# Retention in a hybrid decoder on one core: k of two heads and two gate tiles computed ahead, rotations behind the last norm, and a job's two loads swapped

## The chip, the core and the metric

The kernel runs on one core of one Trainium2 chip. The metric is the device time of one execution in microseconds (us). Five engines work side by side, each through its own instructions in order: TensorE (PE in the profile: matmuls; PEld: its weight loads), VectorE (DVE), ScalarE (ACT), GpSimd (POOL) and SyncE (SP, which here only issues DMAs). ACT and POOL issue a few DMAs as well. An engine that waits for a semaphore holds up everything behind it in its own order.

## The reference, cut to what matters

One step of a decoder of two layers, for 512 prompt tokens and 8 x 4 sample tokens together (544 columns, `T`; `HT` is half of it). Layer 0 mixes by a short gated convolution, layer 1 by retention with 4 heads (`NH`); behind each mixer stands a gated feed-forward network (FFN).

```
def retention_mixer(x, s0, pos, w_in, gn_g, w_out):
    z = x @ w_in
    q, k, v, g = jnp.split(z, [QK_DIM, 2 * QK_DIM, 2 * QK_DIM + V_DIM], axis=-1)
    ...
    q = rotary(q, pos)
    k = rotary(k, pos) * (HEAD_DK ** -0.5)
    o, S = retention_chunkwise(q, k, v, s0)
    of = (of - mu) * lax.rsqrt(var + GN_EPS)
    ...
    out = (jax.nn.silu(g) * of.astype(x.dtype)) @ w_out
```

A head has 256 columns of q and of k (2 pieces of 128 each) and 512 of v and of the gate g (4 gate tiles of 128).

## The kernel before, in words

Activations lie transposed: 128 features on the partitions, 544 tokens along the row. Every fp32 operand is split into a high and a low part (`split`, L191: ACT writes the high part, DVE subtracts), and a product takes three matmuls: high x high, high x low, low x high. Where `split_adding` or `mixed` is used, the low part of some weights is made by a DMA from POOL's queue that adds the weights to the negated high part.

Two forms of a projection stand beside each other. `project` (its matmuls are L175) takes one piece of 128 output columns: 8 row blocks x 3 x 2 halves = 48 matmuls of 272 columns. A `Job` (L461 and on, its matmuls L480) computes two pieces with a scheme of seven products (after Strassen and Winograd): 7 x 4 x 3 = 84 matmuls of 272 columns. Its operands on the activation side are sums made once; on the weight side, `weights7` (L428) loads two blocks, `w3` (L434) and then `w1` (L435), and forms sums on DVE (L438 needs only `w3`, L439 both) that are then split. The seven products go into three banks of PSUM: `begin` makes product 1 and takes it (`u1`), `middle` products 6, 5 and 2 (`u2`, `c11`), then 7 (`u3`, `c22`), `end` the products 4 and 3 (`c21`, `c12`). Each "take" is a small step of ACT (L540 and others) or DVE (L543) that reads a bank, so that it can be written again. `run` (L516) calls, for each job, `prepare` of the next one, `middle`, `begin` of the next one, `end`.

The program has these stages: the convolution; FFN 0, a long chain of jobs; `ahead` (L785); retention, head by head; FFN 1; the final norm. `ahead` computes, still in the pools of FFN 0, what retention needs first: k and q of head 0 by `project`, stored unrotated to DRAM (`qk_made`), and gate tiles as jobs, stored finished to DRAM (`gate_made`): two of head 0, and all four of heads 1 and 2 (`AHEAD`), 5 jobs.

Then the tables `gt` (the decay factors of a head) and the raw k and q of head 0 (`rot`) are loaded back (`qk_start`, L915; `qk_loaded`, L926), issued on SP's queue after `last_load`, the last load of the jobs. DVE scales (L942, L930) and rotates them (`rotate`, L969 to L974: six steps of 128 x 544 for one of q and k).

A head runs so:

- `value` (L987): v in four weight pieces (`c`), each of 24 matmuls of 512 columns (L999 to L1001); behind each odd piece four small matmuls for the sample tokens (L1007). Behind the second piece stand the splits of q and k (`qk_split`), `sample_scores`, the transposes of k (`keys`: L1049, L1058), and, in heads 1 and 2, the split of the previous head's gated output (`held_parts`).
- `fill(0)` to `fill(3)`: blocks of projections between the steps of the recurrence. In heads 1 and 2 these are the output projection of the previous head (`held_project`), in head 0 its gate tiles 2 and 3 and k of head 1, in head 3 its own four gate tiles (`gate_project`).
- `scores`, the sample tokens' states (`sample_outputs`, `states_update`: DVE steps S, L1243), and the outputs of the four chunks (`inner`), each normalized over its 512 columns (`normalized`: mean and variance on DVE, a power on POOL for the reciprocal root, L227, and `yn`, L1148), transposed by PE (L1172) and multiplied into the gate (`gated`, L1178).
- Among these stand projections of the next head: in head 0 both pieces of q of head 1; in heads 1 and 2 the two pieces of k of the next head, and behind the last norm (`yn3`) and its transposes the two pieces of q. A rotation follows the second piece at once. The second piece holds, in its middle (`inside`), a state update and the transposes of `yn2`.
- Head 3 has no next head: its places are taken by the output projection of head 2 (pieces 4 and 5, then 2 and 3 about the last norm), and `last_project` ends the stage.

The order on each engine is written by the order of the calls, with `issue_after` placing a group behind a given instruction; a scheduler and the pools' free slots decide the rest. PE's order is therefore fixed when the program is built.

The functions that the change touches:

Of the kernel before, what the change touches and what calls it, by code (L numbers as in the profile page):

```python
# [12 lines left out]
P = 128  # L13
# [36 lines left out]
def hybrid_decode_kernel(ctx: ExitStack, tc: tile.TileContext, a: dict, o: dict):  # L50
# [79 lines left out]
    last_load = [None]  # L130
# [297 lines left out]
    def weights7(src1, src2, sw, adding=False):  # L428

        n = KP * P  # L430
        w3, w1 = [wts.tile([P, 2 * n], F32, tag="w", name=nm("w")) for _ in range(2)]
        w2 = sw.tile([P, 2 * n], F32, tag="w2", name=nm("w2"))
        w4 = sw.tile([P, n], F32, tag="w4", name=nm("w4"))
        last_load[0] = nc.sync.dma_start(w3, src2)  # L434
        last_load[0] = nc.sync.dma_start(w1, src1)  # L435
# [347 lines left out]
    gate_made = {h: dram.tile([P, 4, T], F32, tag=f"g{h}", name=nm("gm")) for h in (0, *AHEAD)}  # L783

    def ahead(tp, fp, sw, operand_tiles):  # L785

# [46 lines left out]
        def gates(h, n):  # L833
# [28 lines left out]
    with ExitStack() as c2:  # L862
# [47 lines left out]
        def qk_start(h):  # L910

            st = {}
            gt = kp.tile([P, 2, T], F32, tag="gt", name=nm("gt"), bufs=1)
            with tc.issue_after(last_load[0].ins) if h == 0 else ExitStack():
                nc.sync.dma_start(gt, a["gtab"][h])  # L915
            st["gt"] = gt
            st["rot"] = [
                pool.tile([P, 2, T], F32, tag=f"rot{w}", name=nm("rot"), bufs=1) for w, pool in enumerate((tp, kp))
            ]
            return st  # L920

        def qk_loaded(st):

            for t, src in ((st["rot"][1], qk_made[1]), (st["rot"][0], qk_made[0])):
                with tc.issue_after(last_load[0].ins):
                    nc.sync.dma_start(t, src)  # L926
# [16 lines left out]

        def qk_project(h, st, which, dt, inside=None):
# [42 lines left out]
        def value(h, st):  # L987
# [4 lines left out]
            for c in range(4):  # L992
# [19 lines left out]
                if c == 1:  # L1012
# [89 lines left out]
        def gate_project(h, st, n):  # L1102
            st.setdefault("gate", [])
            if h == NH - 1 and n % 2 == 0:

                pool, tag = ((kp, "gt"), (qp, "qkhl1"))[n // 2]
                t = pool.tile([P, 2, T], F32, tag=tag, name=nm("gate"), bufs=1)
                st["gate"].append(t)
            elif not st["gate"]:
                st["gate"].append(swapped(True, [P, 4, T], F32, "gate"))  # L1110
# [27 lines left out]

        def normalized(src, tag="yn"):
# [8 lines left out]
            nc.vector.tensor_scalar(yn, src, mv[:, 0:1], rs, op0=ALU.subtract, op1=ALU.mult)  # L1148
# [149 lines left out]
        for h in range(NH):  # L1298
            more = h + 1 < NH

            def fill(n):
# [4 lines left out]
                elif h:  # L1306
                    gate_project(h, st, n)
# [3 lines left out]
                else:  # L1311
                    qk_project(h + 1, nxt, 1, n - 2)

# [24 lines left out]
            if not more:  # L1338
                held_parts(h, older)
# [6 lines left out]
            if more and h:  # L1346
                nxt = qk_start(h + 1)
                for which in (1, 0):
                    qk_scale(nxt, which)
# [27 lines left out]
            if more and h:  # L1377
                qk_project(h + 1, nxt, 0, 0)
                qk_project(h + 1, nxt, 0, 1)
# [122 lines left out]
```

## Time and profile before

| | |
|---|---|
| Median of 3 runs | 1458.5 us (1458.18 to 1458.96) |
| Profiled execution | 1461.27 us |
| Its span, first to last instruction | 1459.5 us |
| Mean granted TensorE clock | 0.996 |
| PE busy | 1443.8 us (99%) |
| DVE, ACT, POOL busy | 985.7, 664.0, 147.9 us |
| Bytes moved by DMA | 201.89 MB, mean 138 GB/s |

The profile was taken in one execution, whose own time is 2.8 us above the median of the runs; times inside the trace are measured against its span. The columns of the rows quoted below are: in the list of waits, the engine and line that waited, what it waited for, the total, the number and the longest; in the busy times by stage, the stretch, then for each engine the busy time and number of instructions, the granted clock, the DMA share and GB/s; in the timelines, start, duration, engine, line, operation, output tile <- input tiles, shape, and in brackets the idle time ahead of it and what ended it. The matmuls' durations overlap: what a matmul costs is the distance from one start to the next.

### The profile page before, as it was taken

The numbers are of one execution on the slowest core, as the hardware profiler recorded it, in microseconds if no ns is written. First come the engines' busy times: TensorE is split into PE (matmuls) and PEld (weight loads), VectorE is DVE, ScalarE is ACT, GpSimd is POOL, SyncE is SP. The second block draws the span as 40 slices with busy tenths as digits, with TensorE's granted clock in tenths as the row PEclk, the third lists the DMA queues.
The fourth block names the chain that finished last, engine by engine and source line by source line (L and its number), as shares of the span: only waits on it lengthen the run. The fifth ranks groups of instructions, "written<-read, shape, count | busy, mean of one in ns | idle before, by whom it ended". The sixth has DMA issues, their size and how long they took to land.

```text
span 1459.5 us, 26302 instructions
## 1 busy us (share of the span) xinstructions
PE 1443.8 (99%) x10860; PEld 1369.0 (94%) x10860; DVE 985.7 (68%) x1536; ACT 664.0 (45%) x971; POOL 147.9 (10%) x184
## 2 busy tenths in 40 slices
PE   9999999999999999999999999999999999999997
PEld 8999999999999999997878888878999999999997
DVE  5644679847748648677575765845699848749554
ACT  5222466626526437664223032134386626537334
POOL 0100011101101003210010000000111101101002
PEclk9999999999999999999999999999999999999998
DMA  6222246636536434767353734724666635546432
GB/s 219 82 88 92 86 114 140 150 116 126 143 106 139 124 80 133 195 167 262 125 191 116 258 106 144 274 92 143 175 138 149 153 108 131 131 109 148 119 81 77
DMA packets 84297, 201.89 MB, mean 138 GB/s; under 512 B 8129, under 2 KB 25409, under 8 KB 83921
## 3 DMA queue, kind: packets, MB, share of 16 engines
q1 hardware_dynamic: 67296, 165.91, 35.9%
q0 software_dynamic: 15008, 29.18, 12.2%
q10 hardware_dynamic: 1872, 5.12, 0.9%
q8 instruction: 85, 1.39, 0.4%
q14 instruction: 36, 0.29, 0.1%
HBM read 175.11 MB, written 25.08 MB: 137 GB/s over the span
## 4 chain that ended last, share of the span: by engine, by line
PE 89%; DVE 5%; DMA 3%; ACT 1%; issue 1%; POOL 0%; SPq 0%; DVEq 0%; ACTq 0%; POOLq 0%
PE sm L480 35%; PE mm L175 33%; PE sm L175 7%; PE sm L999 2%; PE sm L1000 2%; PE sm L1001 2%; PE sm L163 2%; PE sm L164 1%; PE sm L165 1%; PE sm L1222 1%; DMA w<-in_ffgu_dram 1%; DVE wl L191 1%; DMA w<-in_rtg_dram 1%; DVE S L1243 1%; DVE ol L191 1%
## 5 line engine op out<-in xcount | busy, mean ns | idle before, releaser
L190 ACT ACTIVATE wh<-w 128x1024 fp32r<-128x1024 f32 (+4 forms) x126 | 115.8, 923 | 318.8 <-PE mm L175 204.9
L480 PE MATMUL sm<-oh,wh 128*128 128x272 f32 x744 | 215.5, 290 | 0.1
L480 PE MATMUL sm<-ol,wh 128*128 128x272 f32 x744 | 214.3, 288 | 0.7 <-DVE ol L191 0.7
L480 PE MATMUL sm<-oh,wl 128*128 128x272 f32 x744 | 213.9, 287 | 0.0
L175 PE MATMUL mm<-xh,wh 128*128 128x272 f32 x844 | 176.3, 290 | 1.1 <-ACT wh L190 1.0
L175 PE MATMUL mm<-xh,wl 128*128 128x272 f32 x844 | 174.5, 289 | 0.4 <-DMA wl<-in_rtqk_dram 0.4
L175 PE MATMUL mm<-xl,wh 128*128 128x272 f32 x844 | 173.9, 287 | 0.0
L480 PE MATMUL sm<-oh,h 128*128 128x272 f32 x568 | 164.1, 289 | 0.5 <-DVE gate L543 0.4
L480 PE MATMUL sm<-oh,l 128*128 128x272 f32 x568 | 163.5, 288 | 0.0
L480 PE MATMUL sm<-ol,h 128*128 128x272 f32 x568 | 163.5, 288 | 0.0
L273 DVE TENSOR_TENSOR x<-x,mm 128x544 f32<-128x544 f32 x90 | 64.7, 719 | 144.7 <-PE mm L175 144.7
L191 DVE TENSOR_TENSOR wl<-w,wh 128x1024 fp32r<-128x1024 f32 (+4 forms) x126 | 134.2, 1071 | 23.7 <-ACT wh L190 22.3
L480 PEld LDWEIGHTS sm<-oh,wh 128*128 128x128 f32 x744 | 139.8, 188 | 2.1 <-ACT gate L540 0.9
L423 ACT ACTIVATE wh<-w 128x1024 fp32r<-128x1024 f32 x97 | 102.8, 1060 | 83.2 <-PE sm L480 56.1
L480 PEld LDWEIGHTS sm<-ol,wh 128*128 128x128 f32 x744 | 139.8, 188 | 0.9 <-DVE ol L191 0.9
L480 PEld LDWEIGHTS sm<-oh,wl 128*128 128x128 f32 x744 | 140.3, 189 | 0.0
L426 POOL DMA_DIRECT2D wl<-in_ffgu_dram x87 | 75.6, 869 | 635.2 <-ACT wl L425 261.5
L175 PEld LDWEIGHTS mm<-xh,wh 128*128 128x128 f32 x844 | 132.2, 188 | 5.4 <-ACT wh L190 1.4
L175 PEld LDWEIGHTS mm<-xh,wl 128*128 128x128 f32 x844 | 131.6, 188 | 0.9 <-DMA wl<-in_rtqk_dram 0.6
L175 PEld LDWEIGHTS mm<-xl,wh 128*128 128x128 f32 x844 | 132.1, 188 | 0.1
L191 DVE TENSOR_TENSOR l<-w,h 128x1024 fp32r<-128x1024 f32 x98 | 93.4, 955 | 27.0 <-ACT h L190 26.4
L480 PEld LDWEIGHTS sm<-oh,h 128*128 128x128 f32 x568 | 107.2, 189 | 1.0 <-ACT wh L423 0.6
(296 smaller groups left out, 3211.8 us busy)
## 6 DMA issues: line engine op xcount, KB each, us to landing
w<-in_ffgu_dram SPq DMA_DIRECT2D x88, 512.0 KB, 3.9
wl<-in_ffgu_dram POOLq DMA_DIRECT2D x87, 256.0 KB, 4.8
w<-in_ffdn_dram SPq DMA_DIRECT2D x96, 192.0 KB, 2.5
S<-in_rets_dram SPq DMA_DIRECT2D x16, 1024.0 KB, 7.0
out_rets_dram<-S SPq DMA_DIRECT2D x16, 1024.0 KB, 4.8
w<-in_cvin_dram SPq DMA_DIRECT2D x21, 512.0 KB, 3.4
w<-in_rtqk_dram SPq DMA_DIRECT2D x16, 512.0 KB, 3.6
w<-in_rtg_dram SPq DMA_DIRECT2D x16, 512.0 KB, 4.1
```

Source lines behind the costliest of these rows:

```text
L163: nc.tensor.matmul(out, lh, rh, start=start, stop=False, skip_group_check=True)
L164: nc.tensor.matmul(out, lh, rl, start=False, stop=False, skip_group_check=True)
L175: last_product[0] = nc.tensor.matmul(half(pt, hf)[:, :HT], w[:, c], act[k][:, hf * HT : (hf + 1) * HT], start=(first and k == ks[0] and i ...
L190: h = nc.scalar.activation(dh, src, AF.Copy)
L191: last_low[0] = nc.vector.tensor_sub(dl, src, dh.bitcast(F32))
L273: last_residual[0] = nc.vector.tensor_add(xk, xk, p)
L423: nc.scalar.activation(wh, w, AF.Copy)
L426: nc.gpsimd.dma_start(wl[:, n:], src[:, n:], accum_op=ALU.add)
L480: last = nc.tensor.matmul(out, w[:, c], b, start=(first and k == 0 and i == 0), stop=(k == KP - 1 and i == 2), skip_group_check=True,)
L999: nc.tensor.matmul(out, xh[kt][:, ts_], wh[:, cw], start=(kt == 0), stop=False)
L1000: nc.tensor.matmul(out, xh[kt][:, ts_], wl[:, cw], start=False, stop=False)
L1001: last = nc.tensor.matmul(out, xl[kt][:, ts_], wh[:, cw], start=False, stop=(kt == KT - 1))
```

## The change

- Three more jobs in `ahead`: k of head 2, k of head 3 (`gates(h, None)`: weights of k in place of those of two gate tiles, the raw sums stored to `k_made`), and gate tiles 0 and 1 of head 3. The list is (0,0), (1,0), (1,2), (2,k), (2,0), (2,2), (3,k), (3,0): 8 jobs.
- Heads 1 and 2 project only q of the next head (two pieces, where k stood). The next head's `gt` and raw k are loaded behind `fill(3)`; behind the last norm (`last_norm`, the DVE step of `yn3`) k is scaled and rotated (`k_loaded`), and then q is rotated, in head 0 too.
- Head 3 computes only its gate tiles 2 and 3, in fills 0 and 1. Fill 2 is empty; fill 3 has the split of head 2's gated output and the output pieces 2 and 3, which stood about the last norm.
- In `value`, the splits of q and k, `sample_scores`, `keys` and `held_parts` stand behind the third weight piece, not the second.
- `weights7` loads `w1` first and `w3` second. `gt` and the raw k of head 0 are issued after the last job's first load (`second_load`), q after its second.

Counted over the program: PE has 10646 matmuls in place of 10682, SP 385 DMA issues in place of 382, ACT's queue 16 in place of 13, POOL's 111 in place of 105.

```diff
     def weights7(src1, src2, sw, adding=False):
...
-        w3, w1 = [wts.tile([P, 2 * n], F32, tag="w", name=nm("w")) for _ in range(2)]
+        w1, w3 = [wts.tile([P, 2 * n], F32, tag="w", name=nm("w")) for _ in range(2)]
...
+        second_load[0] = nc.sync.dma_start(w1, src1)
         last_load[0] = nc.sync.dma_start(w3, src2)
-        last_load[0] = nc.sync.dma_start(w1, src1)
...
+            def k(what, src):
+                g = tile2()
+                if what == "c21":
+                    nc.scalar.activation(g[:, 1, :HT], src, AF.Copy)
+                elif what == "c12":
+                    nc.scalar.dma_start(k_made[h], g)
+
+            if n is None:
+                return Job([a["rtqk"][h, 2 + i] for i in range(2)], operand, sw, summed(tile2, k))
             return Job([a["rtg"][h, n + i] for i in range(2)], operand, sw, summed(tile2, gate))
 
-        jobs = [gates(0, 0)] + [gates(h, n) for h in AHEAD for n in (0, 2)]
+        jobs = [gates(*hn) for hn in ((0, 0), (1, 0), (1, 2), (2, None), (2, 0), (2, 2), (3, None), (3, 0))]
...
-            with tc.issue_after(last_load[0].ins) if h == 0 else ExitStack():
+            with tc.issue_after(second_load[0].ins) if h == 0 else ExitStack():
                 nc.sync.dma_start(gt, a["gtab"][h])
...
-                with tc.issue_after(last_load[0].ins):
+                with tc.issue_after((second_load if src is qk_made[1] else last_load)[0].ins):
                     nc.sync.dma_start(t, src)
...
+        def k_loaded(h, st):
+
+            r = st["rot"][1]
+            nc.vector.tensor_mul(r, r, st["gt"][:, 1, :].unsqueeze(1).to_broadcast([P, 2, T]))
+            rotate(r, *products())
...
-            if dt:
+            if dt and which:
                 rotate(r, *products())
...
-                if c == 1:
+                if c == 2:
                     qk_split(h, st, 1)
                     qk_split(h, st, 0)
                     sample_scores(h, st)
...
-                elif h:
-                    gate_project(h, st, n)
                 elif n < 2:
 
                     gate_project(h, st, n + 2)
-                else:
+                elif more:
                     qk_project(h + 1, nxt, 1, n - 2)
+                elif n == 3:
+                    held_parts(h, older)
+                    held_project(h, 2)
+                    held_project(h, 3)
...
             if h in AHEAD:
                 st["gate"] = [swapped(h == 2, [P, 4, T], F32, "gate")]
                 nc.sync.dma_start(st["gate"][0], gate_made[h])
-            if not more:
-                held_parts(h, older)
+                if more:
+                    nxt = qk_start(h + 1)
+                    nc.sync.dma_start(nxt["rot"][1], k_made[h + 1])
+                    for which in (1, 0):
+                        qk_scale(nxt, which)
+            elif not more:
+                st["gate"][0] = qp.tile([P, 2, T], F32, tag="qkhl1", name=nm("gate"), bufs=1)
+                nc.sync.dma_start(st["gate"][0], gate_made[h][:, :2, :])
...
-                    qk_project(h + 1, nxt, int(h > 0), 0)
+                    qk_project(h + 1, nxt, 0, 0)
...
-                qk_project(h + 1, nxt, int(h > 0), 1, inside)
+                qk_project(h + 1, nxt, 0, 1, inside)
             else:
                 held_project(h, 5, single=True)
                 inside()
-                held_project(h, 2, single=True)
             yn3 = normalized(p3)
-            if not more:
-                held_project(h, 3)
+            if more:
+
+                with tc.issue_after(last_norm[0].ins):
+                    if h:
+                        k_loaded(h + 1, nxt)
+                    rotate(nxt["rot"][0], *products())
             gated_pair(h, st, (yns, 4), (yn3, 3))
-            if more and h:
-                qk_project(h + 1, nxt, 0, 0)
-                qk_project(h + 1, nxt, 0, 1)
```

More of the change, by code (lines that the diff above doesn't have):

```diff
@@ L782, in hybrid_decode_kernel @@
     qk_made = [dram.tile([P, 2, T], F32, tag=f"qk{w}", name=nm("qkm")) for w in range(2)]
[L783 removed]
+    k_made = {h: dram.tile([P, 2, T], F32, tag=f"k{h}", name=nm("km")) for h in range(2, NH)}
+    gate_made = {h: dram.tile([P, 4, T], F32, tag=f"g{h}", name=nm("gm")) for h in range(NH)}
     def ahead(tp, fp, sw, operand_tiles):
@@ L1102, in gate_project @@
         def gate_project(h, st, n):
[L1103 to L1110, printed above, removed]
+            if n == 2:
+                last = h == NH - 1
+                t = kp.tile([P, 2, T], F32, tag="gt", name=nm("gate"), bufs=1) if last else swapped(True, [P, 4, T], F32, "gate")
+                st["gate"] = [None, t] if last else [t]
             wh, wl = load_piece(a["rtg"][h, n], KT * P)
```

9 lines of the change are left out of this document (3 added, 6 removed).

## Prediction

> **What bounds the kernel now.** I read the head of the page first, then the list of PE's waits, then the busy times by stage; the chain of waits and the timelines serve for single terms.
>
> ```profile
> span 1459.5 us, 26302 instructions
> PE 1443.8 (99%) x10860; PEld 1369.0 (94%) x10860; DVE 985.7 (68%) x1536; ACT 664.0 (45%) x971; POOL 147.9 (10%) x184
> ```
>
> ```profile
> PE sm L480 <- DVE gate L543: 2.2, 2, 1.8
> PE sm L309 <- DVE expo L103: 1.1, 1, 1.1
> PE mm L175 <- ACT wh L190: 1.0, 1, 1.0
> PE mm L175 <- DMA wl<-in_rtqk_dram: 0.4, 1, 0.4
> ```
>
> TensorE is busy 99% of the span, and the waits shown (us in total, times, longest) come to 4.7 us of some 5.7 named. So time comes from two places only: fewer matmuls, or more and fewer of those waits. The largest wait (L480 on L543) lies in the stage with the jobs that this change lengthens.
>
> ```profile
> core 0: us, PE busy (x) PEld busy (x) DVE busy (x) ACT busy (x) POOL busy (x), PEclk, DMA share, GB/s
> 205.00:548.00 343.00, 342.87 (x2734) 342.22 (x2735) 239.01 (x363) 176.07 (x265) 37.86 (x43) 1.00 0.51 124
> 582.00:655.00 73.00, 70.46 (x534) 68.51 (x533) 52.76 (x86) 48.50 (x76) 11.86 (x12) 0.98 0.69 184
> 760.00:863.00 103.00, 102.92 (x667) 85.30 (x666) 66.84 (x100) 25.75 (x34) 3.60 (x5) 1.00 0.49 166
> ```
>
> These are the first FFN, the stage with the jobs ahead of retention, and the second head. Only the middle one has idle time (2.5 us) and a granted clock under 1. The head has next to none, so whatever starts to wait there is new.
>
> **The gain: 36 matmuls.** A projection of 48 matmuls a piece becomes half a job of 84 for two pieces. Three pairs move: 3 x 96 go, 3 x 84 come. From the chain:
>
> ```profile
> 40.20 11.95 PE sm L175 x96
> 328.48 63.15 PE sm L480 x504
> ```
>
> 11.95/96 = 0.1245 us in a projection, 63.15/504 = 0.1253 in a job. So 288 x 0.1245 - 252 x 0.1253 = **4.3 us less**. That is all the change can take from TensorE's work; about 31.6 us of job work now stands ahead of the heads.
>
> **The jobs ahead.** The largest wait, by SP, DVE and PE:
>
> ```profile
> 625.85 0.33 SPq L435 DMA_DIRECT2D w<-in_rtg_dram  x1
> 626.23 0.43 SPq L915 DMA_DIRECT2D gt<-in_gtab_dram  x1
> 626.70 0.42 SPq L926 DMA_DIRECT2D rot<-qkm  x1
> ```
>
> ```profile
> 629.65 0.69 DVE L439 TENSOR_TENSOR w<-w,w 128x512 f32<-128x512 f32 x1 [1.18 <-DMA w<-in_rtg_dram]
> 631.24 1.36 DVE L942 TENSOR_TENSOR gt<-gt,R 128x544 f32<-128x544 f32 x2 [0.29 <-DMA gt<-in_gtab_dram]
> 633.19 1.29 DVE L930 TENSOR_TENSOR rot<-rot,gt 128x1088 f32<-128x1088 f32 x1 [0.59 <-DMA rot<-qkm]
> 634.40 0.43 DVE L543 TENSOR_TENSOR gate<-gate,sm 128x272 f32<-128x272 f32 x1
> ```
>
> ```profile
> 632.80 0.29 PE L480 MATMUL sm<-oh,wl 128*128 128x272 f32 x1
> 634.88 0.39 PE L480 MATMUL sm<-xh,h 128*128 128x272 f32 x1 [1.80 <-DVE gate L543]
> ```
>
> ```profile
> 636.00:638.00 2.00, 2.00 (x12) 2.00 (x11) 1.75 (x5) 0.63 (x1) 0.02 (x1) 0.51 0.90 130
> 638.00:640.00 2.00, 2.00 (x12) 2.00 (x12) 2.00 (x3) 1.32 (x2) 0.00 (x0) 0.64 0.27 48
> ```
>
> DVE runs in order: its take of a product (L543) stood behind steps that waited for gt and rot. From start to start PE lost 634.88 - 632.80 - 0.125 = 1.96 us. Then the granted clock falls to 0.51 and 0.64 over two stretches of 2 us: 2 x 0.49 + 2 x 0.36 = 1.7 us of clock (counted by matmul starts 1.55, which I take; a half clock lasting 3.4 us fits both). The two waits of 0.4 us in the list (the other one for L543, and the one for rtqk's wl) cost about 0.5 each from start to start, so this stage loses about 4.6 us.
>
> The Trainium skill ("TensorE: Matmul & The Clock Gate", section "What's actually happening") has a free-running window of 3.4 us after at least one idle one of which TensorE falls to half clock. The trace agrees in the length (3.4 us), but 1.80 us of idle time sufficed here. By the rule as stated no wait that I forecast below would halve the clock, by the trace those near 1.80 may; that is the second rival.
>
> In the changed order two places are late. (1) The take of c11 in the first k job stands behind a gate's 128x1088 multiply (1.29 us, as L930's), the splits, and a wl that waits for ACT: DVE needs some 5.5 us where PE covers 4.0, so 1.5 us. (2) The last job's second load goes to SP behind gt and rot: 0.85 us of issue, and two transfers of 557 KB ahead of it. L438, which heads the job's sums, now needs that load (before, only L439 did), and the take of c22 is queued behind L438. DVE has some slack, so 1.5 us again, between 0 and 3. The boundary at 627 keeps 0.5. Against 4.6 before: 3.5, with no half clock, so **-1.1 us**; from -4 (neither is late) to +3 (both, each with a half-clock stretch). The six more accumulating loads on POOL and three stores on ACT's queue ride beside: POOL is busy 11.86 of 73 us.
>
> In the FFN jobs the same L438 comes at most one load (0.33 us of issue and its landing) later; the 343-us row above has 0.13 us idle, so slack is unproven. Counted through the queue order, most takes of c22 keep 0.05 to 0.3 us. I take **+0.2** (0 to 1).
>
> **value's fourth weight piece.** Before, sample_scores, the transposes of keys and their copies stood between the third and the fourth piece; they now come behind the third, and in the new order on PE the fourth follows the third's 24 matmuls (0.235 us apart) with almost nothing between: this cover is gone. In the first head:
>
> ```profile
> 668.35 0.34 SPq L145 DMA_DIRECT2D w<-in_rtv_dram  x1
> 673.67 1.06 ACT L190 ACTIVATE wh<-w 128x1024 fp32r<-128x1024 f32 x1 [0.90 <-DMA w<-in_rtv_dram]
> 674.76 2.50 DVE L191 TENSOR_TENSOR wl<-w,wh 128x1024 fp32r<-128x1024 f32 x2 [0.74 <-ACT wh L190]
> 676.17 0.40 PE L1000 MATMUL sm<-wl,xh 128*128 128x512 f32 x1
> ```
>
> This wl was ready 0.2 us ahead of its reader (674.76 + 1.22 = 675.98). Without the cover PE is there some 1.9 us earlier. The load isn't earlier (it waits for the slot of the first piece, which the xs matmuls read), and it took 5.3 us to land (668.35 to 673.65) beside two more loads: **+1.7 us** (0 if it lands as fast as in the later heads, 3.3 if the wait also halves the clock). There the load takes 3.6 us and ACT, which came to the split 0.66 us late because of the copy of the keys, is free: worked out the same way, wl is 0.25 us late in each of three heads, **+0.7** (0 to 1.5).
>
> **The ends of the heads.** First to second:
>
> ```profile
> 746.79 3.01 POOL L227 TENSOR_TENSOR rs<-rs,expo 128x1 f32<-128x1 f32 x1 [7.34 <-DVE rs L226]
> 749.83 0.81 DVE L1148 TENSOR_SCALAR yn<-sm,mv,rs 128x512 f32<-128x512 f32 x1 [0.44 <-POOL rs L227]
> 750.70 0.66 PE L1172 MATMUL mm<-cb,yn 128*128 128x128 f32 x4
> ```
>
> ```profile
> 828.35 0.54 POOL L227 TENSOR_TENSOR rs<-rs,expo 128x1 f32<-128x1 f32 x1 [8.15 <-DVE rs L226]
> 1037.61 1.39 POOL L227 TENSOR_TENSOR rs<-rs,expo 128x1 f32<-128x1 f32 x1 [7.73 <-DVE rs L226]
> ```
>
> PE reached the transposes of yn3 as they became ready, behind 24 matmuls of the next value. In the new order they stand behind 7: 17 x 0.235 = 4.0 us earlier. The rotation's steps go behind the norm: one of 0.64 us stood in front of rs, three beside POOL's step of 3.01 us, which took 0.54 and 1.39 in other places. With these, 4.0 - 0.6 - 2.5 (or 1.6) = 0.9 to 1.8, less the 0.2 us of slack; unchanged at 3.01, 3.2. **+1.0** (0.7 to 3.2).
>
> The Trainium skill ("GPSIMD Engine Reference", section "Specifications") says that POOL shares its SBUF interfaces with VectorE and contends with DVE steps that have two SBUF inputs. The trace agrees: 3.01 us beside the rotation's two-input steps. By that rule the step is 0.54 and the term 0.7, and the time 0.3 us less.
>
> Second to third and third to fourth:
>
> ```profile
> 837.35 0.81 DVE L1148 TENSOR_SCALAR yn<-sm,mv,rs 128x512 f32<-128x512 f32 x1 [0.43 <-POOL rs L227]
> 838.70 0.72 DVE L973 TENSOR_TENSOR rot<-rot,rt 128x544 f32<-128x544 f32 x1
> ```
>
> Before, 96 matmuls of q (12 us) stood behind the last norm and hid what DVE owed. Now the next value follows at once, while DVE has the k multiply (1.29), twelve rotation steps (12 x 0.64 = 7.6), the gate products and the splits of weights: saturated for about 24 us. PE can wait for yn3 (0.5), for the sample scores (0.2) and for PSUM that the key copies free (0.5). Against about 0.4 us of small waits that go, I take **+0.6 for each, 1.2** (0 to 3).
>
> **The last head.** Two gate projections lay ahead of the scores and two behind; now the two that stay stand ahead, and nothing lies behind.
>
> ```profile
> 998.50 0.42 DVE L1135 TENSOR_TENSOR sf<-sm,cb 128x256 f32<-128x256 f32 x1 [2.15 <-PE sm L165]
> 999.71 0.56 DVE L191 TENSOR_TENSOR sl<-sf,sh 128x384 fp32r<-128x384 f32 x1 [0.59 <-ACT sh L190]
> ```
>
> From scores to sl DVE and ACT need 1.8 us, which PE now covers with some 3 us; but the held projection behind it needs a bank that two state updates (1.2 us each) free. **+1.0** (0 to 2). Then the tail:
>
> ```profile
> 1033.61 0.66 PE L1172 MATMUL sm<-cb,yn 128*128 128x128 f32 x4
> 1039.21 0.81 DVE L1148 TENSOR_SCALAR yn<-sm,mv,rs 128x512 f32<-128x512 f32 x1
> 1041.82 0.60 PE L1172 MATMUL mm<-cb,yn 128*128 128x128 f32 x4
> ```
>
> Between the transposes of yn2 and those of yn3 lay 8.2 us of matmuls, and yn3 was ready at 1040.0, 6.4 us after the first. The two held projections moved to fill 3 leave 4.4 us, and DVE has about 1 us less ahead of the norm: 6.4 - 1.0 - 4.4 = **+1.0** (0 to 2).
>
> **The sum.** -4.3 - 1.1 + 0.2 + 1.7 + 0.7 + 1.0 + 1.2 + 1.0 + 1.0 = +1.4 us on the profiled execution (1461.27 us: the span of 1459.5 and 1.8 around it), so 1462.7 in its terms. It lies 2.8 us above the median of the runs, 1458.5, and I carry the difference over: 1459.9. A measurement of this kernel can tell about 0.2%, 2.9 us, from no change; so this forecast is "the same".
>
> **Rivals.**
> 1. *All the cover holds.* Loads land as fast as in the later heads, POOL's step shrinks, and only the ahead stage keeps its two waits: -4.3 - 1.1 and +0.9 of the rest (0.2 in the FFNs, 0.7 at the first head's end), so -4.5: 1454. For it: 102.92 of 103 us busy in the heads, with ACT at a quarter and DVE at two thirds; against it: wl in the first head had 0.2 us to spare.
> 2. *Slower: the half clock.* A wait that leaves TensorE idle as long as the 1.80 us before 634.88 costs a second time, 1.55 us. Three forecast waits lie a little under that: the two of the ahead stage (1.5) and the fourth piece in the first head (1.7). From 0.3 us more on each, the sum is +1.4 + 0.9 + 3 x 1.55 = +7.0: 1465.5. For it: it happened at 636; against it: two waits of 1.1 and 1.0 us left the clock at 1.00 at the start (the row below), so a shorter wait is free.
>
> ```profile
> 0.00:10.00 10.00, 7.88 (x42) 6.99 (x43) 3.55 (x11) 5.50 (x12) 0.34 (x6) 1.00 0.81 228
> ```
>
> 3. *The change only moves work.* k of the last heads costs the same TensorE time ahead if jobs don't run at 0.125 us a matmul there; the stage before ran its 534 matmuls so outside the waits named, so I give this no chance of its own.
>
> **How the numbers follow.** The forecast, some waits for the gain: 0.42, with 1456 to 1462.5 of its own. Rival 1: 0.28. Rival 2, or DVE's saturation at its upper bounds (3 + 2 + 2 in place of 1.2 + 1.0 + 1.0, so +5.2 in all): 0.30. The range takes in most of both: 1453 to 1466. Faster by over 0.2% (under 1455.6) has nearly all of rival 1 and the forecast's low end: 0.29; slower (over 1461.4) rival 2 and the forecast's high end: 0.33; within 0.38.
>
> **What would show it.** Right: 36 fewer matmuls; in the heads new PE waits at L1017 for wl (1.7 us, then 0.25), at the transposes of yn3, each under 1.5 us; no stretch at 0.50 in the ahead stage. Wrong: a second stretch at half clock (rival 2), PE waits of under 2 us in all (rival 1), or a wait on the raw k or on gate_made's last pair, which I cost at nothing since their stores lie well over 100 us ahead of their loads.

## The result and the profile after

The changed kernel is slower by 0.6%: 1467.45 us (median of 4 runs, 1465.15 to 1469.57) against 1458.34 for the kernel before (1457.49 to 1458.96), a ratio of 1.0063 with a 95% interval of 1.0045 to 1.008. The prediction was 1459.9, its range 1453 to 1466, with "the same" as the likeliest case. The time lies outside the range, on the side of the second rival.

The head of the page and the list of PE's waits (us in total, times, longest) of the changed kernel:

```profile
span 1466.0 us, 26325 instructions
PE 1444.4 (99%) x10824; PEld 1363.6 (93%) x10824; DVE 999.4 (68%) x1559; ACT 675.2 (46%) x994; POOL 147.4 (10%) x190
```

```profile
PE sm L1016 <- ACT wh L190: 1.9, 1, 1.9
PE sm L480 <- DVE gate L543: 1.8, 3, 0.9
PE sm L480 <- ACT gate L852: 1.4, 1, 1.4
PE sm L480 <- DVE wl L424: 1.3, 1, 1.3
PE sm L309 <- DVE expo L103: 1.1, 1, 1.1
PE sm L1188 <- DVE yn L1164: 1.0, 2, 0.5
```

PE has 36 matmuls less: 10824 in place of 10860 (the traces count 178 more in either kernel than the count over the program). It is still busy for 1444.4 us: half-clock matmuls count as busy too, and so does a part of each wait (idle for 1.35 us in the third row, it costs 1.51 from one start to the next). The wait at L309 and one of the three for L543 (0.37 us at 627) stood in the list of before; the others are new.

The kernel before was profiled a second time (the run "e_before" below), and that execution had no half-clock stretch. It is the better base: its span is 1456.6 us, in step with its median (the times lie 1.8 us above the spans). I divide both traces at the same places: the first matmul of the sample tokens (the xs matmul, L1007 or L1024) in each head, and the first and the last matmul of a job in the second FFN. The work that moved is 252 x 0.1253 = 31.6 us into the stage ahead, 11.95 us out of each of heads 2, 3 and 4.

| stretch | before (e_before) | after | less the moved work | forecast |
|---|---|---|---|---|
| start to the first xs matmul (FFN 0, jobs ahead) | 663.98 | 699.53 | +4.0 | -0.9 |
| first head | 89.93 | 93.61 | +3.7 | +2.7 |
| second head | 102.77 | 91.67 | +0.9 | +0.85 |
| third head | 102.69 | 92.14 | +1.4 | +0.85 |
| last head and tail | 115.17 | 104.20 | +1.0 | +2.25 |
| second FFN | 343.42 | 345.68 | +2.3 | 0 (0.2 for both FFNs) |

The sum is +13.1 - 4.3, so about +8.9 us, of the 9.4 by which the spans differ. The gain of 4.3 us came, and the six stretches took it back three times over; three of them carry 10 of the 13 us.

Not all of the first +4.0 belongs to the jobs ahead. Their first matmul starts at 598.06 us here and at 596.40 in e_before, so 1.7 us were lost before it, in small waits on the way. e_norm and e_c1 below, whose edits touch only the heads, start it at 596.68 and 597.94: this part differs from one execution to the next. From that matmul to the first xs matmul the loss beside the moved work is 2.3 us.

The wait of 1.35 us behind L852 (1.51 from start to start), in rows of DVE, ACT and PE of the changed kernel (start, duration, line, output <- input):

```profile
634.31 0.69 DVE L424 TENSOR_TENSOR wl<-w,wh 128x512 fp32r<-128x512 f32 x1 [2.28 <-ACT wh L423]
635.46 1.29 DVE L849 TENSOR_TENSOR gate<-gate,R 128x1088 f32<-128x1088 f32 x1
636.66 1.82 DVE L191 TENSOR_TENSOR l<-w,h 128x512 fp32r<-128x512 f32 x2
638.40 0.68 DVE L441 TENSOR_TENSOR w<-w,w 128x512 f32<-128x512 f32 x1
639.00 0.69 DVE L424 TENSOR_TENSOR wl<-w,wh 128x512 fp32r<-128x512 f32 x1
639.61 0.43 DVE L543 TENSOR_TENSOR gate<-gate,sm 128x272 f32<-128x272 f32 x1
```

```profile
636.78 1.12 ACT L850 ACTIVATE gate<-gate 128x1088 f32<-128x1088 f32 x1
637.80 1.04 ACT L423 ACTIVATE wh<-w 128x1024 fp32r<-128x1024 f32 x1
638.75 1.37 ACT L852 ACTIVATE gate<-gate,vec 128x544 f32<-128x544 f32 x2
```

```profile
638.54 0.29 PE L480 MATMUL sm<-xh,wl 128*128 128x272 f32 x1
640.18 0.36 PE L480 MATMUL sm<-oh,h 128*128 128x272 f32 x1 [1.35 <-ACT gate L852]
```

The list names L852 because that ended last ahead of PE (640.12). In the program PE waits for DVE's take L543, which ended at 640.04. From the multiply that finishes a gate job (L849) to the end of this take DVE runs for 4.6 us without a pause, and PE had matmuls for only 3.2 of them. Nothing in between waits for ACT: L424 needs L423, which ended at 638.84, before L441 did. The wait for ACT lies ahead of the multiply, where DVE was idle for 2.28 us before the L424 at 634.31. So the steps that finish one gate job, late themselves, hold up the next job's first take on DVE.

In the first head, SP's load of the fourth weight piece, its split, and what the clock then did (columns of the last fence: stretch, its length, busy us and instructions of PE, PEld, DVE, ACT and POOL, granted clock, DMA share, GB/s):

```profile
700.66 0.33 SPq L145 DMA_DIRECT2D w<-in_rtv_dram  x1
```

```profile
707.39 1.06 ACT L190 ACTIVATE wh<-w 128x1024 fp32r<-128x1024 f32 x1 [8.57 <-DMA w<-in_rtv_dram]
```

```profile
708.50 0.49 PE L1016 MATMUL sm<-wh,xh 128*128 128x512 f32 x1 [1.85 <-ACT wh L190]
```

```profile
705.00:710.00 5.00, 3.15 (x15) 2.04 (x15) 2.97 (x6) 2.23 (x3) 0.00 (x0) 0.94 0.18 72
710.00:715.00 5.00, 5.00 (x21) 3.74 (x20) 1.30 (x2) 1.23 (x2) 0.00 (x0) 0.72 0.34 105
```

The load took 6.7 us to arrive (5.3 before), PE waited 1.85 us, and the clock lost 5 x 0.06 + 5 x 0.28 = 1.7 us behind it. With the 1.94 us from start to start this makes 3.6 of the 3.7 us of that head.

### The profile page after: what moved, and what is told of

The parts are those of the page before. It is cut to its first block, busy times and chain, and to the rows that moved or that the text cites. A ratio compares the mean times of both kernels' runs of the same rounds, so it can differ in the third digit from the quotient of the medians.

```text
span 1466.0 us, 26325 instructions
## 1 busy us (share of the span) xinstructions
PE 1444.4 (99%) x10824; PEld 1363.6 (93%) x10824; DVE 999.4 (68%) x1559; ACT 675.2 (46%) x994; POOL 147.4 (10%) x190
## 4 chain that ended last, share of the span: by engine, by line
PE 89%; DVE 4%; DMA 3%; issue 1%; ACT 1%; POOL 1%; SPq 0%; DVEq 0%; POOLq 0%; ACTq 0%
PE sm L480 35%; PE mm L175 33%; PE sm L175 7%; PE sm L1016 2%; PE sm L1018 2%; PE sm L1017 2%; PE sm L163 2%; PE sm L164 1%; PE sm L165 1%; PE sm L1238 1%; DVE S L1259 1%; DMA w<-in_rtv_dram 1%; PE mm L1024 1%; PE mm L1188 0%; DMA wl<-in_rtqk_dram 0%
## 5 line engine op out<-in xcount | busy, mean ns | idle before, releaser
L480 PE MATMUL sm<-oh,wl 128*128 128x272 f32 x768 | 220.9, 288 | 1.3 <-DVE wl L424 1.3
L480 PE MATMUL sm<-ol,wh 128*128 128x272 f32 x768 | 221.4, 288 | 0.0
L480 PE MATMUL sm<-oh,h 128*128 128x272 f32 x592 | 171.1, 289 | 1.9 <-ACT gate L852 1.4
L175 PE MATMUL mm<-xh,wh 128*128 128x272 f32 x756 | 157.9, 290 | 0.6 <-ACT wh L190 0.6
L175 PE MATMUL mm<-xh,wl 128*128 128x272 f32 x756 | 156.6, 289 | 0.2 <-DMA wl<-in_rtqk_dram 0.2
L175 PE MATMUL mm<-xl,wh 128*128 128x272 f32 x756 | 155.9, 288 | 0.0
L191 DVE TENSOR_TENSOR wl<-w,wh 128x1024 fp32r<-128x1024 f32 (+4 forms) x120 | 127.3, 1063 | 35.3 <-ACT wh L190 33.5
L423 ACT ACTIVATE wh<-w 128x1024 fp32r<-128x1024 f32 x103 | 109.2, 1060 | 89.2 <-PE sm L480 61.1
L175 PEld LDWEIGHTS mm<-xh,wh 128*128 128x128 f32 x756 | 118.7, 189 | 4.4 <-ACT wh L190 1.1
L175 PEld LDWEIGHTS mm<-xh,wl 128*128 128x128 f32 x756 | 117.9, 188 | 0.9 <-DMA wl<-in_rtqk_dram 0.5
L175 PEld LDWEIGHTS mm<-xl,wh 128*128 128x128 f32 x756 | 118.5, 188 | 0.1
```

What stands on the lines that cost most here:

```text
L175: last_product[0] = nc.tensor.matmul(half(pt, hf)[:, :HT], w[:, c], act[k][:, hf * HT : (hf + 1) * HT], start=(first and k == ks[0] and i ...
L191: last_low[0] = nc.vector.tensor_sub(dl, src, dh.bitcast(F32))
L423: nc.scalar.activation(wh, w, AF.Copy)
L480: last = nc.tensor.matmul(out, w[:, c], b, start=(first and k == 0 and i == 0), stop=(k == KP - 1 and i == 2), skip_group_check=True,)
```

## The experiments

Times are medians; the medians of the kernel before, run beside them, lay at 1458.2 to 1458.6. Line numbers of edited kernels are shifted by up to 17.

**The base.** e_before is the kernel before, unedited.

> The kernel before, unchanged. Its profiled execution lay 2.8 us over the median of its runs, and held one stretch at half clock (1.55 us behind the 1.96-us wait at 632.8). Theory: a typical execution hasn't that stretch, so the base of the prediction was 1.5 to 3 us too high, and the runs' spans should lie near 1456.5 with a mean clock of 0.997 or more. Rival: the distance is noise of the profile, every execution has the stretch, and spans lie at 1459 to 1460 with clock 0.996.

Measured: 1458.8 (10 runs), a profiled span of 1456.6 with a clock of 0.998. Its wait and clock at the place that cost 1.96 + 1.55 us in the first profile:

```profile
PE sm L480 <- DVE gate L543: 1.9, 2, 1.5
```

```profile
630.00:635.00 5.00, 3.50 (x27) 3.28 (x27) 4.28 (x9) 2.04 (x4) 0.88 (x1) 1.00 0.98 299
635.00:640.00 5.00, 5.00 (x42) 4.98 (x41) 5.00 (x9) 4.47 (x7) 0.00 (x0) 1.00 0.48 75
```

The wait is there (1.50 us) and the half clock isn't. The theory holds: the profile that the prediction was made from showed a stretch of 1.55 us that this execution, close to the median, hadn't to give back. Another 1.5 us of the difference lies ahead of the stage (its first job starts at 597.86 there, at 596.40 here).

**Single parts undone.** e_c1 puts the splits back:

```
-                if c == 2:
+                if c == 1:
                     qk_split(h, st, 1)
```

> The changed kernel with the splits of q and k, the sample scores, the keys and held_parts back behind the second weight piece of value. Theory (the lost cover): the 1.85-us wait for the fourth piece in the first head goes with its half-clock stretch (1.94 + 1.55 us), and the 0.4-us one in the third head, so about 3.5 us faster than the changed kernel, 1463.5 to 1464.5. Rival (the third piece was needed): the rotations behind the last norm aren't done by then, PE waits 1 to 3 us per head on the splits, and the time is as the changed kernel's or up to 6 us above.

Measured: 1468.0, no gain in the median. The stretches of the profiled execution tell more: the first head falls from 93.61 to 90.59 us as the theory had it, the stretch up to the first xs matmul rises from 699.53 to 700.50, the last head from 104.20 to 104.87, the second FFN from 345.68 to 347.20. That last is the half clock behind the same 1.3-us wait for L424, in this execution and not in the one of the changed kernel:

```profile
1085.00:1090.00 5.00, 3.56 (x21) 2.92 (x20) 4.95 (x8) 4.02 (x6) 0.54 (x1) 0.91 0.28 46
1090.00:1095.00 5.00, 5.00 (x34) 5.00 (x34) 2.14 (x6) 0.80 (x2) 1.41 (x2) 0.75 0.89 246
```

```profile
1085.00:1090.00 5.00, 3.56 (x24) 2.90 (x23) 4.96 (x10) 4.30 (x6) 0.00 (x0) 1.00 0.38 61
1090.00:1095.00 5.00, 5.00 (x40) 4.86 (x41) 3.49 (x7) 1.40 (x4) 2.08 (x2) 1.00 0.79 218
```

The first pair is e_c1, the second the changed kernel: 1.44 us idle in both, 34 matmuls against 40 in the 5 us behind it. As for the time, neither theory was borne out by this run alone.

e_order undoes the load order:

```
-        w1, w3 = [wts.tile(...) for _ in range(2)]
+        w3, w1 = [wts.tile(...) for _ in range(2)]
-        second_load[0] = nc.sync.dma_start(w1, src1)
-        last_load[0] = nc.sync.dma_start(w3, src2)
+        second_load[0] = last_load[0] = nc.sync.dma_start(w3, src2)
+        last_load[0] = nc.sync.dma_start(w1, src1)
...
-            with tc.issue_after(second_load[0].ins) if h == 0 else ExitStack():
+            with tc.issue_after(last_load[0].ins) if h == 0 else ExitStack():
...
-                with tc.issue_after((second_load if src is qk_made[1] else last_load)[0].ins):
+                with tc.issue_after(last_load[0].ins):
```

> The changed kernel with the loads of a job in the order of before, and the tables of the first head issued behind the last load. Theory (the lost cover of value and the half clock carry the loss): under 1.5 us faster, 1466 to 1467.5. Rival (the load order carries it): the waits on L543 at 656 and 668 (1.1 and 0.7 us) and the 1.5-us one at the start of the second FFN go, 3 us or more faster, 1464 or less.

Measured: 1468.1, between 1464.2 and 1473.3; the profile is of the slowest of the five. In the second FFN the wait goes (343.02 us), but in the stage ahead the wait for the first head's tables comes back (DVE waits 3.3 us for gt, and PE 2.93 us for the take behind it), and PE waits 3.2 us for the fourth weight piece. So the load order has two sides: the rival was right on the second FFN, and neither time was met, since what is won there is lost again.

e_norm puts the rotations back:

```
-            if dt and which:
+            if dt:
                 rotate(r, *products())
...
-                with tc.issue_after(last_norm[0].ins):
-                    if h:
-                        k_loaded(h + 1, nxt)
-                    rotate(nxt["rot"][0], *products())
+                if h:
+                    k_loaded(h + 1, nxt)
```

> The changed kernel with the rotation of q in its old place (behind the projection's second piece) and the rotation of k not held behind the last norm. Theory: the norm's chain on DVE comes later, the waits for yn3 grow from 0.5 to 1 us or more in each of three heads, so 1 to 3 us slower than the changed kernel, 1468.5 to 1470.5. Rival (the rotation behind the norm delays the next value): up to 2 us faster, 1465.5.

Measured: 1467.6 (1464.5 to 1471.5), no difference. The waits for yn3 in heads 2 and 3 grow from 0.74 to 1.09 us from start to start as the theory had it; the one in the first head (0.48) goes, against it. The sum is too small for the spread of these runs.

e_nog3 leaves out the job for the last head's gate tiles:

```
-        jobs = [gates(*hn) for hn in (..., (2, 2), (3, None), (3, 0))]
+        jobs = [gates(*hn) for hn in (..., (2, 2), (3, None))]
```

and gives the last head its four gate projections and the old places of the held ones.

> The changed kernel without the job for the gate tiles of the last head, whose four gate projections stand as before; 12 matmuls more (1.5 us). Theory (each job ahead brings its own waits of 0.7 to 1.1 us in that stage): one wait goes with its job, and the last head gets its cover back (1 us), so as the changed kernel or up to 1.5 us faster, 1466 to 1467.5. Rival (this job is a pure gain): 1.5 us slower, 1469.

Measured: 1474.1, 6.7 us slower than the changed kernel. My theory fell: without the eighth job the waits in the stage ahead don't go, they become others (1.37 and 1.98 us in place of 1.08 and 0.73), and the stage costs the same beside its work (689.16 us and 10.53 for the job, against 699.53). Behind it the clock was halved twice: at 700, as in the profile of the changed kernel, and behind the wait for L424 at 1090, here for 6.8 us, which cost 3.4. With 1.4 us for the 12 matmuls, and 1.2 us that the heads gave back, this makes up the 3.9 us by which this profile, the fastest of the five executions, is longer than that of the changed kernel. Why the median is another 2.5 us above it is not shown.

**The FFNs' load order, and two parts together.** e_ffold keeps the new order only in the stage ahead, e_ffold_c1 has the splits back as well:

```
+    swapped_loads = [False]
...
+        ws = [wts.tile(...) for _ in range(2)]
+        w1, w3 = ws if swapped_loads[0] else ws[::-1]
...
```

The flag is set for the jobs of the stage ahead alone.

> The changed kernel with a job's loads in the old order in both FFNs, in the new order only in the stage ahead of retention. Theory (the load order costs at the start of the second FFN alone): that FFN goes from 345.7 back to 343.0-343.4 us, the stage ahead keeps its four waits, so 2.3 us faster, 1465. Rival (the new order holds the small slack of the first FFN's 20 jobs too): the first FFN changes by 1 us or more as well, 1464 or less; or no gain, since the wait there comes from elsewhere.

> The one of the old load order in the FFNs, and also the splits, sample scores, keys and held_parts behind value's second piece. Theory: the gains add: 2.3 us at the second FFN, 3.0 in the first head, less 0.7 in the last head: 1462.5 to 1463.5. Rival (what one wait gives back another takes, as the first round showed for single edits): 1465 to 1468.

Measured: 1464.1 and 1462.7. The second FFN falls from 345.68 to 343.09 and 343.55 us, and the first shows no new wait with either order: the new order costs at the start of the second FFN, at one wait for L424, and the slack in the first FFN's 20 jobs was enough. All four profiles with the new order there (the changed kernel, e_c1, e_norm, e_nog3) have this wait, at 1.32 us each; no profile with the old order has it. The two parts do add, with 1.5 us for the second where 3.0 was expected.

**The finish of a gate job put off.** In the kernel before and in the changed one, silu, scale and store of a gate job are issued right behind its own last take. These edits issue them only when the next job has come to its third take:

```
                 elif what == "c12":
                     nc.vector.tensor_mul(g, g, r)
-                    nc.scalar.activation(g, g, AF.Silu)
-                    ...
+                    def finish():
+                        nc.scalar.activation(g, g, AF.Silu)
+                        ...
+                    pending.append(finish)
...
+                if what == "u3" and pending:
+                    pending.pop()()
```

and, in e_b_take alone and in e_b_defer with it, the steps of DVE that wait for the first head's tables are placed behind the second-last job's c22:

```
+                with tc.issue_after(takes[-5].ins):
                     qk_scale(st, which)
                     r = st["rot"][which]
                     nc.vector.tensor_mul(r, r, ...)
```

> The kernel before, with the DVE steps that wait for the tables and raw q and k of the first head placed behind the take of the second-last job's c22. Theory: the 1.67-us wait for L543 goes, and with it the half-clock stretch that follows it in some executions (1.55 us): 1.5 to 2.5 us faster than before, 1456 to 1457. Rival: the rotation is then late for the first head's splits, or PE waits for the next take instead: within 1 us of before.

> The kernel before with both the steps for the first head behind the second-last job's c22 (1458.8 by itself) and the finish of the gate jobs put off likewise. Theory: the 1.51-us wait that took the place of the 1.67-us one goes: 1.5 us faster than before, 1457. Rival: a third wait takes its place, within 0.5 us of before.

> The last one (old load order in the FFNs, splits behind value's second piece, 1462.7), and a gate job's finish (silu, scale and store on ACT, 3.6 us) put behind the next job's third take instead of right behind its own last take. Theory (the 1.51-us wait at a job's start is ACT's finish in front of the split that DVE's take is queued behind): that wait goes in the stage ahead, 1.5 to 2 us faster, 1461. Rival (DVE's 1.29-us multiply alone makes it, or the finish stands in front of the next take instead): within 0.7 us, or waits at c22 grow.

Measured: e_b_take 1458.8, no gain: its rival was right. The 1.67-us wait went and the same 1.51-us wait as in the changed kernel took its place:

```profile
PE sm L480 <- ACT gate L851: 1.4, 1, 1.4
PE sm L309 <- DVE expo L103: 1.1, 1, 1.1
PE mm L1060 <- DVE knl L191: 0.4, 1, 0.4
PE sm L480 <- DVE gate L544: 0.4, 1, 0.4
```

With the finish put off too (e_b_defer, 1457.2, ratio 0.999, 0.9981 to 0.9999) no wait is left between the jobs of that stage. The whole list:

```profile
PE sm L309 <- DVE expo L103: 1.1, 1, 1.1
PE mm L175 <- DVE xl L205: 0.3, 1, 0.3
PE mm L175 <- DMA wl<-in_rtqk_dram: 0.2, 1, 0.2
PE sm L175 <- DVE wl L191: 0.2, 1, 0.2
PE sm L731 <- DVE sqacc L218: 0.2, 1, 0.2
```

e_defer, the finish alone put off on top of e_ffold_c1, came to 1459.6: 3.1 us faster, more than I expected. Its stretch up to the first xs matmul falls from 700.21 to 694.94 us; 1.7 of these 5.3 us lie ahead of the first job, so the jobs account for 3.6. The place of a job's finish was thus the cause of most of the waits between the jobs, and in a kernel with 8 jobs it weighs more (3.1 us against 1.6 from e_b_take to e_b_defer). It works by the order of the steps on DVE, not by ACT holding up a split in front of the take, as my theory had it: in e_b_defer the take of c12 no longer stands behind an L424, the multiply starts 5.3 us ahead of the matmul that needs the take (3.2 before), and the take ends 0.26 us ahead of it. Which of the moved steps does it was not tried by itself.

**One job alone.** e_b_g3 is the kernel before with the job for the last head's gate tiles, e_b_g3defer the same with both steps put off:

```
-        jobs = [gates(0, 0)] + [gates(h, n) for h in AHEAD for n in (0, 2)]
+        jobs = [gates(0, 0)] + [gates(h, n) for h in AHEAD for n in (0, 2)] + [gates(3, 0)]
```

and the last head's fills as the change has them.

> The kernel before with one part of the change: the gate tiles 0 and 1 of the last head as a sixth job ahead, its gate tiles 2 and 3 in fills 0 and 1, the split of head 2's output and two held projections in fill 3. k, the rotations, the splits and the load order stay as before. 12 matmuls less: -1.5 us. Theory: one more job start ahead costs 0.5 to 1.5, the last head loses cover (1 us): within 1 us of before, 1457.5 to 1459.5. Rival (this part is free, as 6.7 us lost without it suggest): 1.5 us faster, 1457 or less.

> That part together with the two steps put off in the stage ahead. Theory: -1.5 for the matmuls, -1.5 for the wait, the last head's cover +0.5 to 1: 1456 to 1457, which would beat both kernels. Rival: the waits move on again, 1458 or more.

Measured: e_b_g3 1462.7, worse than either theory: the boundaries of the added job bring waits of 1.51, 0.83 and 2.88 us from start to start. With both steps put off, 1456.0: a ratio of 0.9981 (0.9973 to 0.999). This version beats both kernels, the one before by 2.5 us. Its last head is 103.93 us against 115.17 - 11.95 = 103.22.

**The parts in the heads, without waits ahead of them.** e_cured is e_defer with the old load order everywhere and the first head's steps placed as above; e_cured_norm has the rotations back besides, e_cured_c2 the later splits of the change.

> The changed kernel with three things against its waits: the old load order everywhere (loads of the first head behind the last load), the finish of gate jobs put off, and the first head's steps behind the second-last job's c22; the splits of q and k stay behind value's second piece. Theory (the stage ahead lost by waits that its order made, not by three more jobs): that stage then costs only its 252 matmuls more than the quiet one (31.5 us), so 2 us faster than 1459.6: 1457.5, within 0.2% of before. Rival (three more jobs can't be had without waits): 1459 or more.

> The same with the rotation of q in its old place and that of k not held behind the last norm. Theory: the norm is later by the rotation, the waits for yn3 grow by 0.35 in two heads as the trace of the single edit showed, and the 0.5 in the first head's goes: within 1 us of the one beside it. Rival: the rotation behind the norm is worth 2 us or more to the change: 1459.5 or more.

> The same as the first with the splits, sample scores, keys and held_parts behind value's third piece, as the change has it. Theory: the first head pays 1.4 to 1.9 us for the fourth weight piece, more where the wait halves the clock, and the sample scores' waits of 1.2 us in the third head go: 0.5 to 3 us slower. Rival: no difference within 0.5 us, and the piece's load in the changed kernel was late by chance.

Measured: 1459.7, 1455.9 (ratio 0.9983, 0.9974 to 0.9992) and 1460.9. The whole change of the work is thus to be had at a gain of 2.5 us, in e_cured_norm. But 1.3 of these are e_b_defer's, which moves no work: of the 4.3 us of matmuls the medians show 1.2, no more than e_b_g3defer shows with a third of them. The first waits of e_cured_norm, and those of e_cured:

```profile
PE sm L1205 <- DVE yn L1181: 1.6, 2, 0.8
PE mm L1092 <- DVE knl L191: 1.5, 1, 1.5
PE sm L309 <- DVE expo L103: 1.1, 1, 1.1
```

```profile
PE mm L175 <- DMA wl<-in_rtout_dram: 1.6, 1, 1.6
PE sm L309 <- DVE expo L103: 1.1, 1, 1.1
PE sm L1205 <- DVE yn L1181: 1.0, 2, 0.5
PE mm L175 <- DMA wl<-in_rtqk_dram: 0.9, 1, 0.9
```

Neither theory fits: I had expected under 1 us between these two, and the rival had the version with the rotations back slower; it is 3.7 us faster. But the three heads together differ by only 0.5 us (273.91 against 274.39); most of the rest of this pair of profiles lies in waits for two accumulating loads, of rtout in the tail and of rtqk ahead of the jobs, where no rotation stands. How much of the 3.7 us is the rotation's stays open. e_cured_c2 bears its theory out in the trace: the first head is 92.55 in place of 90.76 us, with 2.27 us of waiting for the fourth weight piece; of that, 1.2 us show in the median.

## Why the prediction was wrong, point by point

- **36 matmuls, -4.3 us.** Right: the heads lost 11.95 us each beside their waits, and without waits an added job costs what its matmuls do: in e_b_g3defer the stretch up to the first xs matmul is 10.59 us longer than in e_b_defer (671.59 against 661.00), for 84 matmuls of 0.1253 us, 10.53. PE's busy time in e_cured_norm, where few waits are left, is 1438.1 us against 1442.2 in e_before and 1441.1 in e_b_defer, 3 to 4 us less.
- **"Against 4.6 before: 3.5, with no half clock, so -1.1 us".** This step failed, above all in its first number. Between the jobs the changed kernel waits 0.53 + 1.51 + 1.08 + 0.73 = 3.85 us from start to start, close to the 3.5 forecast. The kernel before waits 0.53 + 1.67 = 2.20 there in e_before, not 4.6: the 4.6 held a half-clock stretch of 1.55, which that execution doesn't pay, 0.3 more of the longest wait, and 0.5 for rtqk's wl, which was left out of the 3.5 without a reason (the changed kernel has it too, 0.41 us at 592). So the term is +1.65 in place of -1.1, 2.75 us off. It is the largest single part of the miss of 7.5 us; the second FFN adds 2.3, the first head 1.0, and the 1.7 ahead of the first job vary from one execution to the next.

  In (1) the place and the size were right (1.51 us); but the wl that waits for ACT (L424 at 634.31) stands ahead of the multiply, and none between it and the take. Counted from that L424, DVE needs 5.7 us and PE covers 4.4 (5.5 and 4.0 forecast). In (2) the place was right (the take behind L438, 1.5 forecast, 0.73 measured), the reason not: gt and rot left SP at 652. A job's second load is issued when DVE's L441 has read the slot that it takes (SP at 649.49 and 661.93, each just behind an L441), and lands 3.6 to 4.7 us later. The same happens at the job before, which I had not looked at, and costs the 1.08 us:

```profile
649.49 0.33 SPq L435 DMA_DIRECT2D w<-in_rtqk_dram  x1
```

```profile
654.30 0.69 DVE L438 TENSOR_TENSOR w<-w 128x512 f32<-128x512 f32 x1 [2.39 <-DMA w<-in_rtqk_dram]
655.03 0.69 DVE L439 TENSOR_TENSOR w<-w,w 128x512 f32<-128x512 f32 x1
655.64 0.43 DVE L543 TENSOR_TENSOR gate<-gate,sm 128x272 f32<-128x272 f32 x1
```

  The load order is not shown to be the cause here: with the old order (e_order) L439 waits for the late load in place of L438, and the same take costs 0.74 us; the profiles with the new order show 0.54 to 1.31.
- **FFN, +0.2 us.** The first FFN was right (no new wait there). In the second I looked at the takes of the running jobs and not at its start, where the wait for L424 stands: 1.49 us from start to start, more with the half clock. e_ffold shows it to be the load order's.
- **value's fourth piece, +1.7 and 0.7 us.** Right in place, and near in size for the wait (1.94 us), with luck: I had the low part wl as the late one and the load as fast as before, but PE waited already for the high part, since the load took 1.4 us longer. In the six profiles with the later splits this wait is 0.6, 1.3, 1.4, 1.9, 2.3 and 3.2 us. In the third head 0.67 us, in the others less. What I left to a rival, the half clock behind it, came in the profiled execution and made the first head +3.7.
- **The ends of the heads, +1.0 and +1.2 us.** Right in place: 0.48 us from start to start in the first head (half of the forecast), 0.74 in each of the next two (0.6 forecast). POOL's step is 0.54 us in the changed kernel where it was 3.01, now with DVE idle beside most of it (yn at 782.14 waits for it) and the rotation behind:

```profile
781.56 0.54 POOL L227 TENSOR_TENSOR rs<-rs,expo 128x1 f32<-128x1 f32 x1 [6.12 <-DVE rs L226]
```

  The Trainium skill ("GPSIMD Engine Reference", section "Specifications") had POOL contend with DVE steps of two SBUF inputs; this row agrees. So does e_norm: with the rotation back in front of the norm, its steps and a split stand beside POOL's step again, and it takes 3.30 us (at 779.19).
- **The last head and its tail, +2.0 us** (+2.25 with its fourth weight piece). Half of that: 1.0 us, with waits of about 0.3 each at the last two groups of transposes.
- **The second rival, the half clock.** Right as a mechanism, wrong as a limit: I took 1.80 us as the point from which a wait costs a second time. The runs below show none. The price, about 1.55 us, was right for a stretch of 3.4 us; e_order and e_nog3 each have one of twice that length. The changed kernel's four runs spread over 4.4 us where the four of before spread over 1.5, and the slowest has the lowest mean clock (0.996), the fastest the highest (0.998).
- **The base.** I carried the distance of 2.8 us between profile and median over as a constant. In e_before's terms it was a half-clock stretch of 1.55 us and 0.3 us of waiting in the one stage whose gain I was about to forecast, and 1.5 us ahead of it. So the half clock was taken off twice: once as a gain of the change, and once more with the 2.8.

## What to carry to other kernels

Before a profile is used as a base, ask why its execution lies above the median; if the extra time sits in the stage that the change touches, it must not be counted as a gain. Where an engine with 99% busy time is fed by in-order queues, look at each stage's first iteration and at each boundary, and follow the chain through both feeding engines: here the finish of one job came late on DVE, behind a wait for ACT, and so held up the next job's take. Put off what nobody waits for: that alone gave 3.1 us with eight jobs and 1.6 with five, and more jobs ahead paid only in versions that do it.

## What the runs showed of the hardware that I had not expected

The half clock has no threshold that these runs show. It followed idle times of 1.32 us (the second FFN in e_c1 and e_nog3), 1.80, 1.85, 1.97 and 3.17 us (the last two in e_order); it did not follow the same 1.32 us in the changed kernel and e_norm, 1.50 in e_before, 1.82 in e_nog3, 2.27 in e_cured_c2, nor 2.93 us in e_order:

```profile
665.93 0.29 PE L480 MATMUL sm<-oh,wl 128*128 128x272 f32 x1
669.14 0.39 PE L480 MATMUL sm<-xh,h 128*128 128x272 f32 x1 [2.93 <-DVE gate L543]
```

```profile
665.00:670.00 5.00, 2.07 (x17) 1.85 (x16) 1.99 (x4) 1.86 (x3) 1.04 (x2) 1.00 0.97 342
670.00:675.00 5.00, 5.00 (x42) 4.98 (x41) 4.97 (x8) 3.14 (x5) 0.00 (x0) 1.00 0.45 90
```

A wait at the same place of the program, even of the same length, costs it in one profile and not in the next. The Trainium skill ("TensorE: Matmul & The Clock Gate", section "What's actually happening") calls the window free-running, which fits that; it asks for at least one idle window of 3.4 us, and no wait here was so long. Why 2.93 us passed where 1.32 did not is open.

Accumulating loads of 512 KB on POOL's queue took between 5.1 and 8.8 us to land in the tails of these kernels. The last one of the tail cost PE nothing where it took 5.3 us (e_cured_norm) and 1.6 us where it took 6.6 (e_cured), so a part of each comparison of single profiles is luck.
